# An opening rearranged: three weight tiles in step with the input, products of zeros ahead of it, and the squares of the norm between the splits

## The chip, the core and the metric

The kernel runs on one core of one Trainium2 chip. The metric is the device time of one execution in microseconds (us), taken as the median of several runs. The core has a tensor engine (PE) for matrix products, a vector engine (DVE) and a scalar engine (ACT) for elementwise work, and a sync engine (SP) that here only issues transfers (DMA). Each engine works through its own queue strictly in order and waits at an instruction whose input is not there yet.

## The reference, cut to what matters

A state-space mixer (SSD) and an attention mixer (MLA) stand one after the other over 512 tokens of 1024 channels, each with a norm ahead and a residual sum behind, in 32-bit floats.

```python
def rms_norm(x, w):
    xf = x.astype(jnp.float32)
    return (xf * lax.rsqrt(jnp.mean(xf * xf, axis=-1, keepdims=True) + RMS_EPS)).astype(x.dtype) * w
...
def ssd_mixer(u, in_w, conv_w, conv_b, dt_bias, a_log, d_skip, norm_w, out_w):
    proj = u @ in_w
    z = proj[..., :SSM_D_INNER]
    xbc = proj[..., SSM_D_INNER:SSM_D_INNER + SSM_CONV_DIM]
    dt_raw = proj[..., SSM_D_INNER + SSM_CONV_DIM:]
    xbc = jax.nn.silu(causal_depthwise_conv(xbc, conv_w, conv_b)).astype(jnp.float32)
    ...
    dt = jax.nn.softplus(dt_raw.astype(jnp.float32) + dt_bias.astype(jnp.float32))
    a = dt * (-jnp.exp(a_log.astype(jnp.float32)))
    y = ssd_chunked(xs * dt[..., None], a, b_in, c_out)
    y = y + d_skip.astype(jnp.float32)[:, None] * xs
    y = gated_group_rms_norm(y.reshape(bsz, seq, SSM_D_INNER), z, norm_w, SSM_N_GROUPS)
    return y.astype(u.dtype) @ out_w
...
def reference(x, norm_w, ...):
    h = x
    for i in range(DEPTH):          # layer 0: ssd_mixer, layer 1: mla_mixer
        u = rms_norm(h, norm_w[i])
        ...
        h = h + y.astype(h.dtype)
    return rms_norm(h, final_norm_w)
```

## The kernel before

**Tiling.** Channels lie on the 128 partitions and the 512 tokens along the rows, so the input is eight tiles `x[k]` of 128 x 512. The input projection is cut into tiles of 128 output channels; the weights of one tile are 128 x 1024 (eight blocks k of 128 x 128). Every 32-bit operand is split in two parts, a rounded one (`hi`, a cast on ACT) and the rest (`lo`, a subtraction on DVE), and each product is made of three: hi by hi, hi by lo, lo by hi. One projection tile is therefore 8 x 3 = 24 matrix products of 128 x 512.

**Norm.** The norm's factor is the same for all channels of a token, so group 0's projections, and the first four of group 1, are made from `vh`, `vl`, the parts of x times the norm's weight, and multiplied by the factor `r` afterwards. `sumsq` makes `r`: eight squares on ACT (`sq`), summed on DVE (`sqa`), split (`sqh`, `sql`), summed over the partitions by two products with ones (`pssq`), then logarithm, exponential and three DVE steps (`rstd_of`, tile `rr`).

**Groups.** The state-space mixer has eight groups g. The six projection tiles of a group are called B, C, x0, x1, z0 and z1. `ssm_in` makes them, `ssm_evac` applies `r` and the convolution (three shifted multiply-adds, the "taps"), and class `SSD` makes scores (`cb`, `L`), weighted inputs (`xdt`, `xw`), states (`S`) and outputs (`y`). While the group's state-space work runs, the projections of the next group run on PE: the method `sched` weaves small pieces into the stream of products at places given by a table of numbers, in units of PE work. PE's order is thus the order in which the code is written and woven; the order on ACT, DVE and SP is set by a scheduler from the program and its own estimates.

**Weights.** `prefetch` loads a tile's raw weights (pool `wraw`, two buffers, 512 KB each, by SP), and splits them (`whi`, `wlo`, pools of three) up to two tiles ahead. A load waits until the tile that had its buffer is split; a cast into `whi` waits until PE is done with the tile three before. I count weight tiles from 0 in the order of use: 0 to 5 are group 0's, 6 to 11 are group 1's.

**Step sizes (`ssm_dt`).** Sixteen products with the small matrix `wdt` make the raw step sizes (`aux`); times `r` they are `d0`; four products with the identity turn them ("transposes"); then softplus on DVE; then four products that make cumulative sums, copied by ACT to `acT`, stored to DRAM (`ac_d`) and loaded back spread over partitions (`L<-ac_d`).

**The opening.** SP loads `x[0]`, then the first pieces of weight tiles 0 and 1, `x[1]`, `x[2]`, the second pieces, and so on. ACT and DVE split as pieces land; `gemm2` runs tiles 0 and 1 (B and C) in step with the input: per k six products. Then follows tile 2 (x0): six of its products, the sixteen for the step sizes, the two of `pssq`, its other eighteen, and then the four transposes of `d0`. The `link` call in `sumsq` holds all squares back until the last `vh` is made.

Of the kernel before, what the change touches and what calls it, by code (L numbers as in the profile page):

```python
# [33 lines left out]

# Where work is woven into the stream of matrix products, in units of tensor-engine work done since the
# start of the stream (of its share, for SC, TU and PR).
S0P = (13.82, 14.2, 15.4, 15.6, 17.62)  # group 0's projections: dt projection, norm, softplus, raw tiles, cumulative sums
SU = (0.64, 1.42)  # start and spacing of the normalised input tiles
P0 = (6.0, 6.8, 11.91, 15.25, 17.25, 24.88, 32.86, 35.86)  # group 0: sums, decays, cb, x0, x1, states, y0, y1
P1 = (1.0, 2.4, 3.8, 12.0, 16.5, 21.0)  # later groups: cb, x0, x1, states, y0, y1  # L40
GN = 16.84  # gated norm of the group before
G7 = 33.0  # gated norm of the last group
SF = (0.02, 0.1, 2.1, 3.1)  # scores of head 0
SC = (0.0, 0.16, 0.25, 0.44)  # scores of the next head
TU = (0.02, 0.08, 0.38, 0.55)  # transposes of a head's probabilities
PR = (0.3, 0.48, 0.65, 0.94)  # products of a head's probabilities and values
KO = (3, 4, 5, 8, 10)  # steps of the output projection given to the last heads
MID = 4  # projections of group 1 that still use the input without its norm
NU = 1  # projection after which the second norm is worked out
LA = (3, 1)  # heads of a group whose decay exponents the scalar engine takes: groups 0-1, later ones  # L50
OA = 8  # tiles that the output projection splits ahead
SQ = 2


# [88 lines left out]
class Net:  # L143
# [113 lines left out]
    def split_weight(self, raw, cuts=()):  # L257
# [8 lines left out]
        yield hi, lo  # L266

    def mm(self, n=T):
        return self.ps.tile([P, n], F32, tag="mm", name=self.nm("mm"), bufs=3)
# [16 lines left out]
    def gemm2(self, ps, ws, xh, xl, ks):  # L286
        seqs = [self.passes(w, xh, xl, ks) for w in ws]
        for k in range(ks):
            for p, seq in zip(ps, seqs):
                for i in range(3 * k, 3 * k + 3):  # L290
                    self.nc.tensor.matmul(p, seq[i][0], seq[i][1], start=i == 0, stop=i == 3 * ks - 1)  # L291
            yield 6 * 0.216

# [34 lines left out]
    def sumsq(self, tiles, n, pstag, pool=None, tags=("r0", "rt", "rr"), after=None):  # L328
        nc = self.nc
        acc = None  # L330
        for x in tiles:
            sq = self.nrm.tile([P, T], F32, tag="sq", name=self.nm("sq"), bufs=SQ)
            i = nc.scalar.activation(sq[:], x, AF.Square)
            if after is not None:
                self.link(i, [after])
            if acc is None:
                acc = self.nrm.tile([P, T], F32, tag="sqa", name=self.nm("sqa"))
                nc.vector.tensor_scalar(acc[:], sq[:], self.eps_of(n), None, op0=ALU.add)
            else:
                nc.vector.tensor_tensor(acc[:], acc[:], sq[:], op=ALU.add)  # L340
# [10 lines left out]
    def ssm(self):  # L351
# [9 lines left out]
        self.link(self.head, [ld])  # L361
        self.phase, self.group = "E", [self.head]
        raws = [self.wraw.tile([P, D], F32, tag="raw", name=self.nm("raw")) for _ in range(2)]
        self.wload = 2
        for k in range(KD):
# [3 lines left out]
            if k % 2 == 0:  # L369
                s = slice(k * P, (k + 2) * P)  # L370
                for i, raw in enumerate(raws):
                    nc.sync.dma_start(raw[:, s], t["w"][i, :, s])
        wdt = wk.tile([P, KD, NH], F32, name="wdt", bufs=1)
# [9 lines left out]

        vh, vl = [], []
        ws = [self.split_weight(raw, (256, 512, 768)) for raw in raws]
        for k in range(KD):
            a = self.o16.tile([P, T], F32R, tag="o", name=self.nm("vh"))
            b = self.o16.tile([P, T], F32R, tag="o", name=self.nm("vl"))
            last = nc.scalar.activation(a[:], self.xs[k][:], AF.Copy, scale=nw[:, k:k + 1])
            if k % 2 == 0:  # L390
# [6 lines left out]
        for i, w in enumerate(ws):  # L397
            self.wready[self.wq[i]] = next(w)
        self.wpos = 2
        self.ssd_aux = aux  # L400
        box, self.wait = [], []

        def norm0():
            pss = self.sumsq([x[:] for x in self.xs], D, "aux", after=last)
            box.append(self.rstd_of(pss, D))
# [150 lines left out]
    def ssm_in(self, g, uh, ul, early):  # L556
# [3 lines left out]
        for i, (name, ct) in enumerate((("B", 16 + g), ("C", 24 + g), ("x0", 2 * g), ("x1", 2 * g + 1),  # L560
                                        ("z0", 0), ("z1", 0))):
            pair = (0, 1) if g == 0 and i < 2 else (4, 5) if g == NG - 1 and i >= 4 else None
            w = None if pair and i == pair[1] else self.weight("w", U_IN + 6 * g + i)
            xh, xl, r = early[:3] if i < early[3] else (uh, ul, None)
# [5 lines left out]
            if pair:  # L570
                if i == pair[0]:
                    two = [ps, self.mm()]
                    ws = [w, self.weight("w", U_IN + 6 * g + i + 1)]
                    yield from self.gemm2([p[:] for p in two], ws, xh, xl, KD)
                ps = two[i - pair[0]]
            else:
                yield from self.gemm(ps[:], w, xh, xl, KD)
# [486 lines left out]
```

## Time and profile before

| what | value |
|---|---|
| time of the kernel before, median of 3 runs | 843.92 us (843.35 to 844.57) |
| the profiled execution, first to last instruction (span) | 841.8 us |
| what lies around that span, against the median | 2.1 us |
| PE busy in the span | 825.0 us (98%) |
| DVE busy | 641.1 us (76%) |
| ACT busy | 453.2 us (54%) |
| mean granted clock of PE | 0.997 |

The profile has the span of one execution only; its own time as a whole is not in it, so the median less the span, 2.1 us, is taken for what lies around. Rows of a timeline read: start, duration, engine, line, operation, what is written from what, tile size, count, and in brackets the engine's idle time just before and what ended it. In a row of several, the duration is that of the whole row. Two rows that follow each other on one engine overlap by some tens of nanoseconds, since an instruction's record begins before the one ahead has left the engine; so what one costs in a stream is the distance of two starts and not its own duration.

### The profile page before, as it was taken

What the parts mean: (1) busy time and instruction counts of PE and PEld (TensorE: products, weight loads), DVE (VectorE), ACT (ScalarE), POOL (GpSimd) and SP (SyncE); (2) the same over time, 40 slices, a digit from 0 to 9 for tenths busy, and PEclk for the clock granted to TensorE, in tenths of its full rate; (3) what the DMA queues carried; (4) which work ended last, traced back from release to release, by engine and by line L of the source; (5) the groups of instructions that cost most, each with busy time, mean ns of one, the idle gap of its engine ahead of it and who ended that gap; (6) DMA issues with size and microseconds to landing.
All of it is one profiled execution on the core that took longest, in us unless ns stands there. A gap on an engine that the chain in (4) does not pass through costs nothing.

```text
span 841.8 us, 11569 instructions
## 1 busy us (share of the span) xinstructions
PE 825.0 (98%) x4260; PEld 694.9 (83%) x4260; DVE 641.1 (76%) x1226; ACT 453.2 (54%) x802; POOL 0.2 (0%) x4
## 2 busy tenths in 40 slices
PE   6999999999999999999999999999999999999996
PEld 5887888888888888888888888888888888888885
DVE  6999898888887979877465787776867869675544
ACT  7567755545455647334354564457547557553233
POOL 0000000000000000000000000000000000000000
PEclk9999999999999999999999999999999999999998
DMA  6354533434332424332224332122221224321212
GB/s 225 104 175 152 160 131 113 124 122 127 104 126 101 150 76 125 113 122 82 99 100 152 102 116 75 56 86 66 77 65 54 88 71 162 100 93 59 89 62 100
DMA packets 35112, 90.55 MB, mean 108 GB/s; under 512 B 4784, under 2 KB 6320, under 8 KB 35056
## 3 DMA queue, kind: packets, MB, share of 16 engines
q1 hardware_dynamic: 34336, 88.77, 32.6%
q10 hardware_dynamic: 720, 1.05, 0.3%
q8 instruction: 33, 0.54, 0.3%
q14 instruction: 23, 0.19, 0.1%
HBM read 83.12 MB, written 4.33 MB: 104 GB/s over the span
## 4 chain that ended last, share of the span: by engine, by line
PE 90%; DVE 4%; DMA 3%; ACT 2%; issue 1%; SPq 0%; DVEq 0%; ACTq 0%
PE mm L282 53%; PE ot L934 10%; PE s L786 5%; PE mm L291 4%; PE po L828 4%; PE mm L766 3%; PE pt L810 2%; PE yd L132 2%; PE yo L127 1%; PE aux L105 1%; DMA x<-in_x_dram 1%; PE aux L77 1%; PE aux L89 1%; PE yd L282 1%; PE yo L282 1%
## 5 line engine op out<-in xcount | busy, mean ns | idle before, releaser
L263 ACT CAST whi<-raw 128x1024 fp32r<-128x1024 f32 (+3 forms) x132 | 126.9, 965 | 178.7 <-PE mm L282 141.7
L264 DVE TENSOR_TENSOR wlo<-raw,whi 128x1024 fp32r<-128x1024 f32 (+3 forms) x132 | 146.8, 1115 | 52.0 <-ACT whi L263 51.8
L282 PE MATMUL mm<-ah,whi 128*128 128x512 f32 x384 | 153.8, 400 | 0.0
L282 PE MATMUL mm<-ah,wlo 128*128 128x512 f32 x384 | 150.1, 391 | 0.4 <-DVE wlo L264 0.4
L282 PE MATMUL mm<-al,whi 128*128 128x512 f32 x384 | 149.7, 390 | 0.0
L282 PE MATMUL mm<-vh,whi 128*128 128x512 f32 x224 | 89.6, 400 | 1.6 <-ACT whi L263 1.6
L282 PE MATMUL mm<-vh,wlo 128*128 128x512 f32 x224 | 87.8, 392 | 0.7 <-DVE wlo L264 0.7
L282 PE MATMUL mm<-vl,whi 128*128 128x512 f32 x224 | 87.5, 390 | 0.0
L282 PEld LDWEIGHTS mm<-ah,wlo 128*128 128x128 f32 x384 | 72.1, 188 | 16.1 <-DVE wlo L264 0.8
L282 PEld LDWEIGHTS mm<-ah,whi 128*128 128x128 f32 x384 | 72.2, 188 | 15.2 <-issue 1.0
L282 PEld LDWEIGHTS mm<-al,whi 128*128 128x128 f32 x384 | 72.2, 188 | 14.4 <-DVE al L303 0.3
L934 PE MATMUL ot<-whi,ah 128*128 128x512 f32 (+1 forms) x136 | 52.3, 384 | 0.0
L934 PE MATMUL ot<-whi,al 128*128 128x512 f32 (+1 forms) x136 | 51.4, 378 | 0.0
L934 PE MATMUL ot<-wlo,ah 128*128 128x512 f32 (+1 forms) x136 | 51.4, 378 | 0.0
L282 PEld LDWEIGHTS mm<-vh,wlo 128*128 128x128 f32 x224 | 42.0, 188 | 10.8 <-DVE wlo L264 1.5
L282 PEld LDWEIGHTS mm<-vh,whi 128*128 128x128 f32 x224 | 42.1, 188 | 10.0 <-ACT whi L263 1.8
L214 ACT ACTIVATE p<-p,st 128x128 f32<-128x128 f32 (+1 forms) x64 | 36.1, 564 | 25.0 <-DVE st L798 24.8
L282 PEld LDWEIGHTS mm<-vl,whi 128*128 128x128 f32 x224 | 42.2, 188 | 7.2
L814 ACT CAST ph<-pt 128x512 fp32r<-128x512 f32 (+1 forms) x64 | 26.4, 421 | 33.5 <-PE pt L810 33.1
L282 PE MATMUL mm<-ch,whi 128*128 128x512 f32 x104 | 42.6, 409 | 0.0
L282 PE MATMUL mm<-ch,wlo 128*128 128x512 f32 x104 | 40.8, 393 | 0.0
L282 PE MATMUL mm<-cl,whi 128*128 128x512 f32 x104 | 40.7, 392 | 0.0
(231 smaller groups left out, 1649.0 us busy)
## 6 DMA issues: line engine op xcount, KB each, us to landing
raw<-in_w_dram SPq DMA_DIRECT2D x100, 512.0 KB, 3.2
L<-ac_d SPq DMA_DIRECT2D x32, 256.0 KB, 4.1
E<-ea_d SPq DMA_DIRECT2D x32, 128.0 KB, 3.2
raw<-in_ua_dram SPq DMA_DIRECT2D x8, 512.0 KB, 3.3
raw<-in_ub_dram SPq DMA_DIRECT2D x8, 320.0 KB, 2.9
x<-in_x_dram SPq DMA_DIRECT2D x8, 256.0 KB, 4.5
res<-in_x_dram SPq DMA_DIRECT2D x8, 256.0 KB, 3.1
hd<-ht SPq DMA_DIRECT2D x8, 256.0 KB, 2.4
```

The costliest lines, as they stand in the source:

```text
L132: nc.tensor.matmul(yd[64 * h:64 * h + 64, s], self.xdt[j][:, c, h, :], self.L[2 * j + h][:, s], start=True, stop=True)
L214: i = self.nc.scalar.activation(out, in_, func, **k)
L263: nc.scalar.copy(hi[:, a:b], raw[:, a:b])
L264: nc.vector.tensor_tensor(lo[:, a:b], raw[:, a:b], hi[:, a:b].bitcast(F32), op=ALU.subtract)
L282: self.nc.tensor.matmul(ps, a, b, start=i == 0, stop=i == len(seq) - 1)
L291: self.nc.tensor.matmul(p, seq[i][0], seq[i][1], start=i == 0, stop=i == 3 * ks - 1)
L766: nc.tensor.matmul(ps[:, c2 * 256:(c2 + 1) * 256], a, b, start=i == 0, stop=i == 5)
L786: nc.tensor.matmul(ps[:, :n], x[:, s], y[:, :n], start=k == 0, stop=k == 4)
L810: nc.tensor.transpose(pt[:, (b - kb) * P:(b - kb + 1) * P], probs[h][b][:, kb * P:(kb + 1) * P], self.ident)
L814: nc.scalar.copy(ph[:, :n], pt[:, :n])
L828: nc.tensor.matmul(po[:, kb * P:], x, y, start=kb == 0 and k == 0, stop=kb == NCH - 1 and k == 2)
L934: nc.tensor.matmul(ps[:, a:b], x, y, start=start and i == 0, stop=stop and i == 5)
```

## The change

Four things change, all in the opening; the tables that weave the work, S0P among them, stay.

- A tile `idle` of 128 x 128 zeros is written by DVE at the start, and PE multiplies it by itself seven times into a buffer that nobody reads, ahead of everything else.
- Weight tile 2 joins tiles 0 and 1: four more loads of 128 KB stand among the first on SP (its raw data lies in tiles of the pool `act` that are free then), four more narrow splits on ACT and DVE, and `gemm2` now runs three tiles in step, nine products for each k. The wide load and split of tile 2 go.
- The squares of the norm are each linked to the `vh` three later instead of the last one, so they can stand among the splits.
- The cost that `gemm2` reports for a step is now by the number of tiles. The pieces of table S0P fall due where that sum passes them.

```diff
+WARM = 7
...
+    def split_first(self, raw):
+        nc = self.nc
+        hi = self.whi.tile([P, D], F32R, tag="hi", name=self.nm("whi"))
+        lo = self.wlo.tile([P, D], F32R, tag="lo", name=self.nm("wlo"))
+        for k, part in enumerate(raw):
+            s = slice(2 * k * P, 2 * (k + 1) * P)
+            nc.scalar.copy(hi[:, s], part)
+            nc.vector.tensor_tensor(lo[:, s], part, hi[:, s].bitcast(F32), op=ALU.subtract)
+            yield
+        yield hi, lo
...
-            yield 6 * 0.216
+            yield 3 * len(ws) * 0.216
...
-        for x in tiles:
+        for k, x in enumerate(tiles):
...
-                self.link(i, [after])
+                self.link(i, [after[k]])
...
+        idle = wk.tile([P, P], F32, name="idle", bufs=1)
+        nc.vector.memset(idle[:], 0.0)
+        pw = aux()
+        for _ in range(WARM):
+            nc.tensor.matmul(pw[:, :P], idle[:], idle[:], start=True, stop=True)
         raws = [self.wraw.tile([P, D], F32, tag="raw", name=self.nm("raw")) for _ in range(2)]
-        self.wload = 2
+        raws = [[raw[:, 2 * k * P:2 * (k + 1) * P] for k in range(KD // 2)] for raw in raws]
+        third = [self.act.tile([P, T], F32, tag=g, name=self.nm("raw")) for g in ("ah", "al")]
+        raws.append([third[k // 2][:, (k % 2) * 2 * P:(k % 2 + 1) * 2 * P] for k in range(KD // 2)])
+        self.wload = 3
...
-                    nc.sync.dma_start(raw[:, s], t["w"][i, :, s])
+                    nc.sync.dma_start(raw[k // 2], t["w"][i, :, s])
...
-            pss = self.sumsq([x[:] for x in self.xs], D, "aux", after=last)
+            pss = self.sumsq([x[:] for x in self.xs], D, "aux", after=[marks[min(k + 3, KD - 1)] for k in range(KD)])
...
-            pair = (0, 1) if g == 0 and i < 2 else (4, 5) if g == NG - 1 and i >= 4 else None
-            w = None if pair and i == pair[1] else self.weight("w", U_IN + 6 * g + i)
+            pair = (0, 1, 2) if g == 0 and i < 3 else (4, 5) if g == NG - 1 and i >= 4 else None
+            w = None if pair and i != pair[0] else self.weight("w", U_IN + 6 * g + i)
...
-                    two = [ps, self.mm()]
-                    ws = [w, self.weight("w", U_IN + 6 * g + i + 1)]
+                    two = [ps] + [self.mm() for _ in pair[1:]]
+                    ws = [w] + [self.weight("w", U_IN + 6 * g + k) for k in pair[1:]]
```

How the rows move is shown at three places. Line numbers are those of each kernel's own file, so they differ by 12 to 20 between the two; a word in brackets names the engines or transfers whose signals a row waits for. First PE, at the end of the opening: `pssq` is the sum of squares over partitions, `d` is `d0`, `mm_246` is tile 2 (x0), `yd` tile 3 (x1). Before:

```order
L347 MATMUL pssq_306<-sqh_302,onesr 128x512 [waits Activation_49]
L348 MATMUL pssq_306<-sql_303,onesr 128x512 [waits DVE_49]
L282 MATMUL mm_246<-vh_146,whi_188 128x512
...
L282 MATMUL mm_246<-vh_178,wlo_189 128x512
L495 MATMUL aux_358<-ident,d_323 128x128 [waits DMAHW2_49,DVE_49]
L495 MATMUL aux_358<-ident,d_323 128x128 x3
L282 MATMUL yd_400<-vh_130,whi_242 128x512
```

and now:

```order
L507 MATMUL aux_296<-vl_205,w_291 128x512
L359 MATMUL pssq_344<-sqh_340,onesr 128x512 [waits Activation_49]
L360 MATMUL pssq_344<-sql_341,onesr 128x512 [waits DVE_49]
L515 MATMUL aux_371<-ident,d_355 128x128 [waits DMAHW6_49,DVE_49,PE_49]
L515 MATMUL aux_371<-ident,d_355 128x128 x3
L294 MATMUL yd_420<-vh_146,whi_215 128x512
```

The eighteen products of tile 2 that stood between `pssq` and the transposes of `d0` now stand ahead of both; nothing stands between any more. (The number of rows and their order behind the transposes are the same in both, down to the second group's products.)

Second ACT, at the logarithm that begins `r` (`r<-pssq`). Before, one wide cast (tile 4) stood between `sqh` and it; now two do, those of tiles 4 and 5 (`whi_416`, `whi_454`), the second of which waits for its own load:

```order
L264 CAST whi_215<-raw_211 128x1024 [waits DMAHW2_49,PE_49]
L356 CAST sqh_340<-sqa_315 128x512 [waits DVE_49]
L264 CAST whi_416<-raw_213 128x1024 [waits DMAHW3_49,PE_49]
L264 CAST whi_454<-raw_414 128x1024 [waits DMAHW4_49,PE_49]
L215 ACTIVATE r_56_347<-pssq_344 128x512 [waits PE_49]
```

Third DVE, at the split of tile 10 (z0 of group 1): `L` and `cb` are the scores of group 0, `x` and `xdt` the taps and weighted inputs. Before:

```order
L626 TENSOR_SCALAR L_638<-L_638,ac 128x128 [waits DMAHW0_49,DVE_49]
L626 TENSOR_SCALAR L_638<-L_638,ac 128x128 x3
L79 TENSOR_TENSOR cb_713<-aux_708,con 128x512 [waits PE_49]
L264 TENSOR_TENSOR wlo_749<-raw_677,whi_748 128x1024 [waits DMAHW7_49,Activation_49]
L81 TENSOR_TENSOR L_617<-L_617,cb_713 128x512 [waits DVE_49,Activation_49]
L81 TENSOR_TENSOR L_624<-L_624,cb_713 128x512 [waits Activation_49]
```

and now:

```order
L82 TENSOR_TENSOR L_658<-L_658,cb_733 128x512
L622 SCALAR_TENSOR_TENSOR x_134_751<-raw_752,cols,x_134_751 128x511 [waits Activation_49]
L93 TENSOR_TENSOR xdt_763<-aux_758,dt 128x512 [waits PE_49]
L622 SCALAR_TENSOR_TENSOR x_134_751<-raw_752,cols,x_134_751 128x510 [waits DVE_49]
L95 TENSOR_TENSOR xw_665<-xdt_763,dec 128x3x128 [waits DVE_49]
L622 SCALAR_TENSOR_TENSOR x_134_751<-raw_752,cols,x_134_751 128x509 [waits DVE_49]
L265 TENSOR_TENSOR wlo_769<-raw_697,whi_768 128x1024 [waits DMAHW3_49]
```

The `lo` part of tile 10 has moved back past the four `L` products, the three taps of x0, one `xdt` and one `xw`. PE's products of that tile stand where they stood, and the third of them reads `wlo`.

More of the change, by code (lines that the diff above doesn't have):

```diff
@@ L382, in ssm @@
         nc.vector.tensor_copy(self.onesr[:], self.ones)
-        vh, vl = [], []
-        ws = [self.split_weight(raw, (256, 512, 768)) for raw in raws]
+        vh, vl, marks = [], [], []
+        ws = [self.split_first(raw) for raw in raws]
         for k in range(KD):
@@ L388, in ssm @@
             b = self.o16.tile([P, T], F32R, tag="o", name=self.nm("vl"))
-            last = nc.scalar.activation(a[:], self.xs[k][:], AF.Copy, scale=nw[:, k:k + 1])
+            marks.append(nc.scalar.activation(a[:], self.xs[k][:], AF.Copy, scale=nw[:, k:k + 1]))
             if k % 2 == 0:
@@ L398, in ssm @@
             self.wready[self.wq[i]] = next(w)
-        self.wpos = 2
+        self.wpos = 3
         self.ssd_aux = aux
```

## The prediction

> **What bounds the kernel now.** First the page's first part and the list of what PE waited for in the first 110 us:
>
> ```profile
> span 841.8 us, 11569 instructions
> PE 825.0 (98%) x4260; PEld 694.9 (83%) x4260; DVE 641.1 (76%) x1226; ACT 453.2 (54%) x802; POOL 0.2 (0%) x4
> ...
> PE mm L291 <- ACT whi L263: 4.8, 1, 4.8
> ...
> PE yo L127 <- DVE E L135: 0.2, 1, 0.2
> PE aux L495 <- DVE d L491: 0.2, 1, 0.2
> ```
>
> PE bounds the whole; a change in the opening counts by what it does to PE's idle time there and as far as its wake reaches. Then the timeline of PE in the opening, and the chain that ended last, from `pssq` on:
>
> ```profile
> 4.78 0.80 PE L291 MATMUL mm<-vh,whi 128*128 128x512 f32 x1 [4.78 <-ACT whi L263]
> 7.15 0.63 PE L291 MATMUL mm<-vh,wlo 128*128 128x512 f32 x1
> 7.58 0.59 PE L291 MATMUL mm<-vh,whi 128*128 128x512 f32 x1
> 8.00 0.40 PE L291 MATMUL mm<-vl,whi 128*128 128x512 f32 x1
> 8.24 0.40 PE L291 MATMUL mm<-vh,wlo 128*128 128x512 f32 x1
> 18.92 0.50 PE L282 MATMUL mm<-vh,whi 128*128 128x512 f32 x1 [1.41 <-ACT whi L263]
> 20.18 0.50 PE L282 MATMUL mm<-vh,wlo 128*128 128x512 f32 x1 [0.53 <-DVE wlo L264]
> ...
> 25.25 0.24 PE pssq L348
> 25.52 0.61 ACT r L214
> ...
> 28.99 0.70 DVE d L491
> ...
> 29.73 0.66 PE aux L495 x4
> 30.39 5.46 PE yd L282 x24
> ```
>
> Products start 0.43 us apart until 8.00 and 0.23 after it: PE begins at half speed. It loses 1.94 us at tile 2's wide split (1.41 and 0.53). From `pssq` to the end of `d0` it takes 29.69 - 25.52 = 4.17 us, in which PE works on the eighteen products of tile 2 and idles 0.16. A product in the stream costs 5.46 / 24 = 0.2275.
>
> Behind that, DVE sets the pace, as its rows show:
>
> ```profile
> 29.60 1.87 DVE L598 TENSOR_TENSOR raw<-mm,rr 128x512 f32<-128x512 f32 x3
> 31.39 0.74 DVE L602 SCALAR_TENSOR_TENSOR B<-raw,cols,B 128x511 f32<-128x511 f32 x1
> 32.05 0.74 DVE L602 SCALAR_TENSOR_TENSOR C<-raw,cols,C 128x511 f32<-128x511 f32 x1
> 37.74 1.21 DVE L264 TENSOR_TENSOR wlo<-raw,whi 128x1024 fp32r<-128x1024 f32 x1
> 38.87 0.21 DVE L510 TENSOR_SCALAR dy<-de 128x128 f32<-128x128 f32 x1
> 62.89 0.74 DVE L417 SCALAR_TENSOR_TENSOR u<-x,cols,rr 128x512 f32<-128x512 f32 x1
> 65.64 0.88 DVE L626 TENSOR_SCALAR L<-L,ac 128x128 f32<-128x128 f32 x4 [2.01 <-DMA L<-ac_d]
> 67.04 1.21 DVE L264 TENSOR_TENSOR wlo<-raw,whi 128x1024 fp32r<-128x1024 f32 x1
> ```
>
> It works without a pause of note from 29.60 to 63.63, waits 2.01 for `L`, and goes on; the 67.04 row is tile 10. PE meets that queue here:
>
> ```profile
> 72.88 0.39 PE L282 MATMUL mm<-ah,wlo 128*128 128x512 f32 x1
> 79.21 1.56 PE L105 MATMUL aux<-xw,BT 128*128 128x256 f32 x6 [1.19 <-DVE xw L94]
> 81.61 0.50 PE L282 MATMUL mm<-ah,wlo 128*128 128x512 f32 x1 [0.37 <-DVE wlo L264]
> ```
>
> 72.88 is the product that reads tile 10's `lo`: made by 68.2, it is early by 4.7 us. Behind 100 us PE waits for almost nothing.
>
> **The change, part by part.** *The opening.* The first input and weight piece are ahead of all else as before, so real work still starts at 4.78. The zeros are seven products of 128 columns in full 32-bit floats, of which four (eight records, since each runs in two) are this row:
>
> ```profile
> 53.37 1.05 PE L531 MATMUL aux<-con,a 128*128 128x128 f32 x8
> ```
>
> So they take 1.8 us, or 3.7 at half speed, and PE's 4.8 us of waiting at the start covers them, as DVE's idleness there covers the writing of the tile: they cost nothing, and if they lift the clock the 0.43 spacing goes. To the end of `pssq` PE now has 72 + 16 + 2 = 90 products, 90 x 0.2275 = 20.5, so 25.3 if nothing is late. Late is the second input tile, by one piece of 128 KB, which takes 0.4 us at the rate of these slices:
>
> ```profile
> 6.00:7.00 1.00, 1.00 (x4) 0.81 (x3) 0.14 (x1) 0.90 (x2) 0.00 (x0) 1.00 1.04 351
> ```
>
> and then its `vh` and `vl` (0.7 each): nine fast products of k = 0 are done before that, which I put at 0.9 us of waiting. From then on a pair of k brings 0.92 MB, 2.6 us at that rate, for 18 products of 4.1 us: PE is ahead no more. `pssq` ends at 26.2 (25.3 without the wait; if the zeros don't help, 3.2 us at half speed cost 1.5, of which 0.9 hides in the wait: 26.8). Squares and sums end near 21.3 and don't hold it.
>
> *The chain to d0.* The 1.94 of tile 2 is gone, but the eighteen products that covered the 4.17 are ahead of `pssq` now, so all of it is bare. And the logarithm stands on ACT behind tile 5's cast, whose load waits until tile 3 is split, which waits until PE is done with tile 0:
>
> ```profile
> 19.30 1.03 ACT L263 CAST whi<-raw 128x1024 fp32r<-128x1024 f32 x1
> 20.24 1.15 ACT L333 ACTIVATE sq<-x 128x512 f32<-128x512 f32 x2
> ...
> raw<-in_w_dram SPq DMA_DIRECT2D x100, 512.0 KB, 3.2
> raw<-in_w_dram SPq DMA_DIRECT2D x5, 512.0 KB, 4.0
> ```
>
> PE leaves tile 0 after 66 products: 4.78 + 0.9 + 66 x 0.2275 = 20.7; cast 0.95 (20.24 - 19.30), split 1.13 (38.87 - 37.74): 22.8; load 3.2 to 4.0, I take 3.6, the middle of the two rows: 26.4; cast: 27.4. So the logarithm starts at 27.4 and not at 26.2, and `d0` ends at 27.4 + 4.17 = 31.6 against 29.69: **1.9 us later** (without the gate 30.4). PE stands still for 5.4 us.
>
> *The queue of DVE to tile 10.* From the end of `d0` PE needs 72.88 - 29.69 = 43.2 us to the product that reads tile 10's `lo`, and the order of PE's rows there is unchanged. DVE has to do, up to and with that split: 29 scalar-tensor-tensor operations of some 512 columns (taps and `u`) at 32.05 - 31.39 = 0.66, 19.1; 5 wide splits at 1.13, 5.7; 23 tensor-tensor operations at 0.61 (1.87 for three overlapped ones), 14.0; the softplus chain and other small ones, 6.0; the `L` row 0.8; one `xw` 0.5. Sum 46.1. The same prices give 33.8 for the work from 29.60 to the end of the row at 62.89, measured 33.95. Add 0.9 of waits for ACT, which before were filled with the taps of x0 and two splits: 47.0. Then `L`:
>
> ```profile
> 54.62 0.58 ACT L535 COPY acT<-aux 128x512 f32<-128x512 f32 x1
> 55.23 3.88 DMA ac_d<-acT
> 56.32 0.68 DVE L598 TENSOR_TENSOR raw<-mm,rr 128x512 f32<-128x512 f32 x1
> ```
>
> `acT` began 24.9 after `d0`; now it stands on ACT behind B's cast, which waits for that `raw` row, at 25 in the new queue, so 25.8; and the store stands behind one more 512 KB load (up to 1.5 us). `L` came 35.95 after `d0`; I take 36.8 to 38.3, against DVE's arrival at 36.2: 0.6 to 2.1 of waiting, 1.2 taken. Tile 10's `lo` is ready 47.0 + 1.2 = 48.2 after `d0`, PE needs it after 43.2: **a new wait of 5.0 us** (0.4 of it already at the cumulative sums, for `acT`). It ends at 31.6 + 48.2 = 79.8, against 72.88: PE is 6.9 late.
>
> *What that wait absorbs.* The waits at `xw` (1.19), tile 11's split (0.37) and `yo` (0.18) vanish, since DVE is through with them when PE arrives: -1.7. One split (tile 14) now stands ahead of the first `y` and can hold the second `yd` for 0 to 0.6: +0.3. PE's later work is unchanged.
>
> Sum: 6.9 - 1.7 + 0.3 = **+5.5 us**: a span of 847.3, and with the 2.1 around it (843.92 less 841.8) **849.4**. Lower bounds (no waiting in the opening, no gate, `L` and ACT in time, 0.5 off the queue): `d0` at 29.5, 45.6 behind it, 75.1, so 2.2 - 1.7 = +0.5. Upper: `d0` 32.5, queue 49.1, +0.6, one cold clock: +9.1.
>
> **The rivals.** *The clock falls in the gaps.* At the end of the program the clock halves after the last product:
>
> ```profile
> 833.67 0.28 PE L934 MATMUL ot<-wlo,ah 128*128 128x256 f32 x1
> 836.00:837.00 1.00, 0.00 (x0) 0.00 (x0) 0.77 (x3) 0.67 (x2) 0.00 (x0) 1.00 0.07 29
> 837.00:838.00 1.00, 0.00 (x0) 0.00 (x0) 0.00 (x0) 0.17 (x1) 0.00 (x0) 0.72 1.02 375
> ```
>
> 0.72 is a fall at 837.44, 3.5 us after the last product's end. The gaps of 5.4 and about 5 are longer. A cold start costs 3.2 us at 0.43, 1.5 us; behind the first gap it only shortens the second wait, behind the second it adds: 850.9. [...] From the rows alone: one gap of that length stands in the trace, at the end, and there the clock fell; but only a fall behind the second gap costs, and its 4.6 at the split itself is not much over 3.5. I give this 0.23.
>
> *A lighter queue.* No gate on the logarithm (a load that lands in 3.2 behind an early tile 3) and `L` in time: `d0` 30.4, 47.0, so 77.4 and +3.1: 847.0. For it: idle DMA at 22 us; against: tile 5's cast is ahead in the order whatever the load does. 0.17.
>
> *Faster.* DVE reaches tile 10's split within 43 us of `d0`, so that PE never waits there. Then only the start counts: +0.7 (no gate) - 1.7 = -1.0: 842.9. It decides if the 47.0 is 4 too many, which the 0.15 error of the check speaks against; for it, DVE has nothing else to do while `d0` is late. 0.05.
>
> *The zeros don't lift the clock.* `pssq` and what hangs on it 0.6 later: 850.0. 0.06.
>
> **How the numbers follow.** Likeliest 849.4, chance 0.49; its own range 847.6 to 851.2. A measurement here tells 0.2%, 1.7 us, from no change. Slower by more: 0.49 + 0.23 + 0.17 + 0.06 less 0.03 for their lower ends, 0.92; within: 0.04; faster 0.04. The range for eight in ten reaches from the lighter queue with some of its bounds to the cold clock: 845.5 to 852.5.
>
> **What would show it.** In the profile after: products 0.23 apart from 4.8 on; no wait at a wide split near 19; a wait of some 5 us at the transposes of `d0` (released by DVE `d`), the logarithm behind ACT's cast and not `pssq`; a wait of 4 to 5 us near 75, released by DVE `wlo`; none at `xw`. It is wrong if the transposes run before 30.4, if DVE's split of tile 10 ends less than 44 us after `d0`, or if PE's rows turn out to be woven otherwise.

## The result, and the profile after

The changed kernel takes 852.18 us (median of 4 runs, 851.36 to 853.46) against 844.25 (843.35 to 845.19) of the kernel before on the same chip: a ratio of 1.0096, 95% interval 1.0083 to 1.0109, that is 7.9 us slower. The prediction was 849.4, in a range from 845.5 to 852.5. The profiled execution took 852.48 us, its span is 850.7 against 841.8.

The page of the kernel after begins:

```profile
span 850.7 us, 11606 instructions
PE 832.4 (98%) x4274; PEld 702.0 (83%) x4274; DVE 642.5 (76%) x1230; ACT 454.0 (53%) x805; POOL 0.2 (0%) x4
```

PE is busy for 7.4 us more than before: 3.4 of them are the zeros, in time in which PE waited before, and the rest is PE at half clock (granted clock 0.50 from 30.87 to 37.69 and from 82.07 to 85.48, and products 0.43 us apart for longer at the start), since no other product was added. What PE waited for up to 110 us, after (line and operation, releaser, us in total, times, longest):

```profile
PE aux L515 <- issue: 5.1, 1, 5.1
PE mm L294 <- DVE wlo L265: 3.5, 1, 3.5
...
PE yd L133 <- DVE y L138: 0.5, 1, 0.5
```

The two waits that the prediction named are there, at the transposes of `d0` (5.1; "issue" means that the profile shows no releaser, but the wait ends 0.1 us behind `d0`, and in e3 it is put down to DVE `d`) and at tile 10's `lo` (3.5). The waits at tile 2's split, at `xw`, at tile 11 and at `yo` are gone. The timeline of PE, after:

```profile
1.05 3.36 PE L379 MATMUL aux<-idle 128*128 128x128 f32 x14 [1.05 <-DVE eps L334]
4.90 0.80 PE L303 MATMUL mm<-vh,whi 128*128 128x512 f32 x1 [0.50 <-ACT whi L275]
...
9.82 0.63 PE L303 MATMUL mm<-vh,wlo 128*128 128x512 f32 x1
10.25 0.48 PE L303 MATMUL mm<-vh,whi 128*128 128x512 f32 x1
10.57 0.39 PE L303 MATMUL mm<-vl,whi 128*128 128x512 f32 x1
...
27.82 0.40 PE L360 MATMUL pssq<-sql,onesr 128*128 128x512 f32 x1
33.36 1.08 PE L515 MATMUL aux<-ident,d 128*128 128x128 f32 x4 [5.14 <-issue]
...
78.29 0.39 PE L294 MATMUL mm<-al,whi 128*128 128x512 f32 x1
82.15 0.79 PE L294 MATMUL mm<-ah,wlo 128*128 128x512 f32 x1 [3.47 <-DVE wlo L265]
82.74 0.63 PE L294 MATMUL mm<-ah,whi 128*128 128x512 f32 x1
83.17 0.63 PE L294 MATMUL mm<-al,whi 128*128 128x512 f32 x1
...
88.82 1.46 PE L106 MATMUL aux<-xw,BT 128*128 128x256 f32 x6
```

Products of the opening stay 0.43 apart until 10.25 and not until 8.00 as before, in spite of the zeros, and they are 0.43 apart once more behind the second wait. The timeline of ACT, after:

```profile
28.16 1.04 ACT L264 CAST whi<-raw 128x1024 fp32r<-128x1024 f32 x1 [3.07 <-DMA raw<-in_w_dram]
29.11 0.59 ACT L215 ACTIVATE r<-pssq 128x512 f32<-128x512 f32 x1
```

and of DVE, after:

```profile
32.57 0.69 DVE L511 TENSOR_TENSOR d<-aux,rr 128x512 f32<-128x512 f32 x1
...
71.57 0.88 DVE L646 TENSOR_SCALAR L<-L,ac 128x128 f32<-128x128 f32 x4 [1.03 <-DMA L<-ac_d]
...
73.62 0.68 DVE L618 TENSOR_TENSOR raw<-mm,rr 128x512 f32<-128x512 f32 x1
...
80.88 1.22 DVE L265 TENSOR_TENSOR wlo<-raw,whi 128x1024 fp32r<-128x1024 f32 x1
```

The logarithm stands behind tile 5's cast, and `d0` ends at 33.3. From 73.62 to 80.88 DVE does 7.3 us of work that the kernel before did behind that split; tile 10's `lo` is ready at 82.1, 48.8 after `d0` (38.6 before: 68.25 less 29.68).

All of it adds up at one instruction, the product that reads `xw` (L106; L105 before). From its start to the end of the span it is 762.6 us before and 761.9 after. It starts at 88.82 in place of 79.21, +9.61: the transposes are 3.63 later (33.36, 29.73); from them to tile 10 PE needs 45.32 in place of 43.15 with its clock at 0.50 from 30.87 to 37.69, +2.17; the wait is 3.47; from there to L106 it needs 6.67 in place of 5.14, at 0.50 from 82.07 to 85.48, +1.53; and the wait of 1.19 at `xw` is gone.

### The profile page after: what moved, and what is told of

Its sections match the earlier page's. It is cut to its first block, busy times and chain, and to the rows that moved or that the text cites. A ratio compares the mean times of both kernels' runs of the same rounds, so it can differ in the third digit from the quotient of the medians.

```text
span 850.7 us, 11606 instructions
## 1 busy us (share of the span) xinstructions
PE 832.4 (98%) x4274; PEld 702.0 (83%) x4274; DVE 642.5 (76%) x1230; ACT 454.0 (53%) x805; POOL 0.2 (0%) x4
## 4 chain that ended last, share of the span: by engine, by line
PE 89%; DVE 5%; DMA 2%; ACT 2%; issue 1%; SPq 0%; ACTq 0%; DVEq 0%
PE mm L294 51%; PE ot L954 10%; PE mm L303 6%; PE s L806 5%; PE po L848 3%; PE mm L786 2%; PE pt L830 2%; PE yd L133 2%; PE aux L106 1%; PE yo L128 1%; DVE wlo L265 1%; PE yd L294 1%; PE aux L78 1%; PE aux L90 1%; DVE x L622 1%
## 5 line engine op out<-in xcount | busy, mean ns | idle before, releaser
L264 ACT CAST whi<-raw 128x1024 fp32r<-128x1024 f32 (+2 forms) x123 | 123.0, 1001 | 188.7 <-PE mm L294 141.8
L265 DVE TENSOR_TENSOR wlo<-raw,whi 128x1024 fp32r<-128x1024 f32 (+2 forms) x123 | 142.6, 1161 | 60.2 <-ACT whi L264 60.0
L294 PE MATMUL mm<-vh,whi 128*128 128x512 f32 x216 | 86.3, 399 | 0.0
L294 PE MATMUL mm<-vh,wlo 128*128 128x512 f32 x216 | 84.6, 392 | 0.1
L294 PE MATMUL mm<-vl,whi 128*128 128x512 f32 x216 | 84.4, 391 | 0.0
```

The lines of the kernel that those rows point to most:

```text
L264: nc.scalar.copy(hi[:, a:b], raw[:, a:b])
L265: nc.vector.tensor_tensor(lo[:, a:b], raw[:, a:b], hi[:, a:b].bitcast(F32), op=ALU.subtract)
L294: self.nc.tensor.matmul(ps, a, b, start=i == 0, stop=i == len(seq) - 1)
```

## The experiments

Each was run beside the kernel before. From its own trace come the end of `d0`, the place of tile 10's split on DVE (counted in instructions from `d0`), the end of that split, the wait of PE for it, and the start of L106 (the line's number shifts by a few between kernels). Times are medians.

| kernel | time, us | ratio (95%) | `d0` | place | split ends | wait | L106 |
|---|---|---|---|---|---|---|---|
| before (first 3 runs; 843.8 to 844.3 beside the others) | 843.92 | | 29.7 | 65 | 68.3 | 0 | 79.2 |
| after | 852.18 | 1.0096 (1.0083–1.0109) | 33.3 | 81 | 82.1 | 3.5 | 88.8 |
| after, again (e10) | 852.19 | 1.0100 (1.0086–1.0113) | 32.5 | 81 | 82.0 | 4.5 | 89.8 |
| split early (e1) | 847.44 | 1.0037 (1.0025–1.0049) | 31.9 | 68 | 74.3 | 0 | 84.0 |
| cover (e2) | 846.32 | 1.0026 (1.0017–1.0035) | 32.1 | 63 | 69.0 | 0 | 81.4 |
| no zeros (e3) | 853.80 | 1.0125 (1.0109–1.0141) | 33.7 | 81 | 83.2 | 3.8 | 90.0 |
| two tiles (e4) | 844.87 | 1.0010 (1.0002–1.0019) | 31.9 | 65 | 69.8 | 0 | 80.8 |
| logarithm first (e5) | 852.72 | 1.0105 (1.0092–1.0118) | 31.6 | 81 | 80.9 | 4.1 | 88.9 |
| e5, split behind `d0` (e11) | 844.99 | 1.0015 (1.0006–1.0024) | 31.0 | 60 | 67.0 | 0 | 81.0 |
| two tiles, dt first (e6) | 841.82 | 0.9975 (0.9965–0.9984) | 29.2 | 65 | 66.9 | 0 | 77.8 |
| e6, split behind `d0` (e9) | 850.53 | 1.0083 (1.0070–1.0097) | 28.1 | 83 | 79.2 | 3.2 | 87.0 |
| e9, split asked early (e12) | 843.36 | 0.9995 (0.9987–1.0004) | 27.9 | 66 | 66.8 | 0 | 78.4 |
| zeros only (e7) | 842.75 | 0.9992 (0.9983–1.0000) | 29.4 | 65 | 66.4 | 0 | 77.6 |
| squares only (e8) | 845.21 | 1.0019 (1.0010–1.0027) | 30.4 | 65 | 69.2 | 0 | 80.1 |

In every trace L106 to the end of the span is 761.1 to 763.3 us, so to within some 2 us what an experiment does to the time is what it does to that start. "The planner" in the expectations is the scheduler that sets the order on ACT, DVE and SP.

### Tile 10's split in its old place (e1_early_split)

```diff
                 at = P0[2:]
+                pieces.append((11.0, lambda: self.prefetch(11)))
```

> The changed kernel, with one piece added that asks for tile 10's split while the products of tile 8 run, so that in VectorE's order the split comes 13 rows earlier (it leaves the four products of L with cb, C's and x0's taps and two splits of the normalised input behind it). Nothing else moves on TensorE. My theory (the order of VectorE's queue behind d0 sets a second wait, and the clock falls in it): some 7 us less stand ahead of the split, so that it ends near 75 in place of 82.1; TensorE is there at 78.7 and does not wait; the 3.5 us wait and the cold products behind it (1.8) go; the waits at xw return with about 0.5. Time 846.5 to 848. Rival (VectorE as a whole is behind by that much, whatever its order): the wait only moves to the products that read xw, S or y, and the time stays at 851 to 853. Rival (the loss is the 5.1 us at the transposes and nothing else): 852, with TensorE's second wait gone but the same amount lost elsewhere.

847.44, as the first theory had it. What PE waited for, e1:

```profile
PE aux L516 <- issue: 5.2, 1, 5.2
...
PE aux L106 <- DVE xw L95: 0.2, 1, 0.2
```

and the split on DVE, e1:

```profile
73.08 1.22 DVE L265 TENSOR_TENSOR wlo<-raw,whi 128x1024 fp32r<-128x1024 f32 x1
```

The first gap is as long as ever; the second is gone, and 4.7 us with it. PE's order is that of after, and near the split little else moved: its cast on ACT and a few neighbours. So this run is the cleanest measure of what the split's place costs. Some 3 us are left against the kernel before, with the late `d0` and the bare gap, which this run keeps. The rival that VectorE's lateness only moves elsewhere falls for most of it: small waits come back at `cb` (0.8), `S` (0.5) and `xw` (0.2).

### Work between pssq and the transposes (e2_cover)

```diff
-S0P = (13.82, 14.2, 15.4, 15.6, 17.62)
+S0P = (13.82, 14.2, 15.4, 15.6, 24.0)
```

> The changed kernel with the last number of S0P at 24.0 in place of 17.62: the transposes of d0 are put behind all 24 products of tile 3 (yd) in place of ahead of them, so that these products stand between pssq and the transposes, as tile 2's do in the kernel before. The planner then also puts tile 10's split 22 rows earlier in VectorE's order. My theory: d0 still ends near 33.3; TensorE works from 28.2 to 33.7 and its 5.1 us wait goes, with the half clock behind it; it comes to tile 10 near 72.5 to 74, and the split is ready near 72 to 73, so that the second wait is below 1 us; time 843.5 to 846. Rival (VectorE's work behind d0 sets the end whatever TensorE does ahead of it): the second wait grows by the 5 us that the first loses, and the time stays at 851 to 853. Rival (the first gap costs its 5.1 us and the second wait stays): 846.5 to 848 with a wait of 3 us or more at tile 10.

846.32, a little over the expected range. What PE waited for, e2:

```profile
PE aux L551 <- DVE a L545: 3.7, 1, 3.7
...
PE aux L106 <- DVE xw L95: 0.7, 1, 0.7
```

The 5.1 at the transposes is gone, but 3.7 comes back at the cumulative sums: with the transposes asked for later the scheduler puts softplus behind the taps of x0 and x1. L106 starts 7.4 earlier than after, and tile 10's split, 18 instructions nearer to `d0`, is part of it; so this run changes two things at once.

### Without the zeros (e3_no_zeros)

```diff
-WARM = 7
+WARM = 0
```

> The changed kernel without the seven products of zeros (the tile is still written); TensorE has nothing to do until the first input. My theory after the traces (the zeros lift no clock; the clock rises at the end of the first of its windows that real products fill): same time as with them, 851 to 853, products 0.43 us apart for 3 to 7 us from 4.8 on. Rival (the zeros fill part of a window and bring the rise forward by one window of 3.4 us on average in some runs): 1 to 1.5 us slower, 853 to 854. Rival (the zeros are in the way): faster.

853.80, the number of the first rival: some 2 us between the two ratios (1.0125 and 1.0096, whose intervals just touch). PE, e3:

```profile
7.54 0.63 PE L303 MATMUL mm<-vh,whi 128*128 128x512 f32 x1
7.96 0.50 PE L303 MATMUL mm<-vl,whi 128*128 128x512 f32 x1
...
26.70 0.40 PE L360 MATMUL pssq<-sql,onesr 128*128 128x512 f32 x1
```

and ACT, e3:

```profile
22.36 0.62 ACT L356 CAST sqh<-sqa 128x512 fp32r<-128x512 f32 x1 [1.37 <-DVE sqa L352]
22.89 2.00 ACT L264 CAST whi<-raw 128x1024 fp32r<-128x1024 f32 x2
28.56 1.04 ACT L264 CAST whi<-raw 128x1024 fp32r<-128x1024 f32 x1 [3.67 <-DMA raw<-in_w_dram]
```

But this trace does not show that the zeros are the reason. The clock rose at 8.2, behind a window from 4.76 that was 3.42 us busy, and 2.2 us earlier than in after, and `pssq` ended at 27.1, 1.1 earlier; `d0` came 0.4 later all the same. Without the zeros the scheduler put tile 3's cast behind `sqh` (22.89 is the casts of tiles 3 and 4), so tile 5's load came no earlier with the products, and the logarithm stood 2.4 us behind `pssq` in place of 0.9 (at 29.51: ACT, idle from 24.89, first took the cast ahead of it in its queue, at 28.56). The run changes two things, and what the zeros bring in the changed kernel stays open.

### Two tiles in step (e4_two_tiles)

```diff
-            pair = (0, 1, 2) if g == 0 and i < 3 else ...
+            pair = (0, 1) if g == 0 and i < 2 else ...
-        third = ...
-        raws.append(...)
-        self.wload = 3
+        self.wload = 2
-        self.wpos = 3
+        self.wpos = 2
```

> The changed kernel with two tiles in step in place of three: tile 2 is loaded whole and computed behind the pair as in the kernel before, its last 18 products behind pssq; the zeros, the squares among the splits and the loads in pieces stay. My theory (the third tile in step takes the cover from the chain to d0, and through VectorE's order makes the second wait; zeros and squares cost nothing): 843 to 845.5, no wait of over 1 us at the transposes. Rival (the squares among the splits or the zeros delay the opening): 846 or more, with d0 later than 31. Rival (the squares early are a gain by themselves): below 843.

844.87: taking back the third tile takes back 7 of the 8 us. On DVE tile 10's split has its old place, and L106 starts at 80.8. PE at tile 2's split, e4:

```profile
20.23 0.79 PE L294 MATMUL mm<-vh,whi 128*128 128x512 f32 x1 [2.24 <-ACT whi L264]
```

The clock fell in this wait of 2.24 us, and the granted clock was 0.50 from 20.06 to 23.47, which no theory had.

### The parts alone on the kernel before (e7_zeros_only, e8_squares_only)

```diff
+        idle = wk.tile([P, P], F32, name="idle", bufs=1)
+        nc.vector.memset(idle[:], 0.0)
+        pw = aux()
+        for _ in range(7):
+            nc.tensor.matmul(pw[:, :P], idle[:], idle[:], start=True, stop=True)
```

> The kernel before with the seven products of zeros added and nothing else. My theory (zeros count as work for the clock: it rises at the end of the first of its 3.41 us windows that is filled to more than some 80%, which is between 4 and 7 us with them and near 8 without, except where the window's edge falls badly): products 0.23 us apart from 4 to 7 us on; the wait for tile 2's split grows by part of what is won, since it is set by loads and ScalarE; time 843 to 844.3, that is 0 to 1 us faster. Rival (zeros do nothing for the clock): the same time, products 0.43 us apart until 8. Rival (the longer wait at tile 2 then lets the clock fall): up to 1.5 us slower.

842.75: zeros bring some 0.7 us by the ratio, anything from nothing to 1.4 by its interval. The clock rises at 5.2, and the wait for tile 2's split is 1.26 + 0.53. The 80% was an estimate: in the traces the clock did not rise behind windows 2.51 and 2.91 us busy of 3.41 (after; 74% and 85%) and rose behind one of 2.92 (e2).

```diff
-                self.link(i, [after])
+                self.link(i, [after[k]])
```

with the marks of the change as `after`.

> The kernel before with the squares of the norm tied to the input three tiles on, as in the change, in place of all behind the last one; nothing else. My theory (the squares are not what pssq waits for, in either kernel; earlier they only share ScalarE and VectorE with the splits): 843.5 to 845, pssq within 0.6 us of 25.25. Rival (the squares hold up pssq, so that it comes earlier now): d0 1 us or more earlier, 842 to 843. Rival (they delay the splits that the pair waits for): pssq a microsecond or more later, 845 to 846.

845.21, 1.6 us slower by the ratio (0.8 to 2.3), so the second rival was the better one: ACT begins tile 2's cast at 18.52 in place of 17.84, with two more squares ahead of it, and `d0` ends 0.7 later. PE, e8, where a wait of 1.41 stood before:

```profile
19.60 0.50 PE L282 MATMUL mm<-vh,whi 128*128 128x512 f32 x1 [1.77 <-ACT whi L263]
```

### The logarithm ahead of tile 5's cast (e5_log_first, e11_log_first_split_behind)

```diff
+            if self.wpos == 5:
+                self.link(c, [self.last])      # c: the cast; last: the exponential of r
```

> The changed kernel with one order forced on ScalarE: tile 5's cast stands behind the two steps of the norm (logarithm, exponential) in place of ahead of them, so that the logarithm waits for pssq alone. My theory (the cast gates the logarithm by about 0.9 us, and VectorE's queue, which starts with d0, carries every delay of d0 to tile 10): d0 ends 3.6 to 4.2 us after the end of pssq in place of about 5.1, the wait at the transposes falls from 5.1 to about 4.2, and the time by 0.9: 850.5 to 852 beside some 852.5 of the changed kernel. Rival (the queue behind d0 is held by ScalarE or by L, so that d0 earlier by 0.9 brings nothing): no change, the wait at tile 10 unchanged at its clock time.

852.72, no gain. DVE, e5:

```profile
28.44 0.69 DVE L328 TENSOR_TENSOR rt<-rt,r 128x512 f32<-128x512 f32 x1
29.05 1.22 DVE L267 TENSOR_TENSOR wlo<-raw,whi 128x1024 fp32r<-128x1024 f32 x1
30.19 0.68 DVE L329 SCALAR_TENSOR_TENSOR rr<-rt,r 128x512 f32<-128x512 f32 x1
```

The logarithm started 0.03 behind `pssq`, but the same tile's split on DVE now stood between two steps of the norm and took 1.1 us back. So that split was sent behind `d0` too:

```diff
+            if self.wpos == 5:
+                self.link(v, [self.d0])        # v: the subtraction; d0: the product that makes d0
```

> The changed kernel with two orders forced: on ScalarE tile 5's cast behind the logarithm and the exponential, as in the experiment with the logarithm first, and on VectorE tile 5's split behind d0 in place of between the norm's second and third step, where it stood in that experiment (29.05, 1.2 us). My theory (that split took back what the logarithm had won): d0 ends 4.1 to 4.3 us after the end of pssq in place of 5.1 to 5.2, the wait at the transposes is 4.2, and the time is 0.8 to 1.2 below that of the changed kernel, near 851.3. Rival (the queue behind d0 is held by ScalarE or by L, not by d0): d0 earlier, the wait at tile 10 longer by as much, no gain.

844.99, where I had expected 851.3. `d0` ended 4.2 us behind `pssq`, as expected, 0.6 earlier than in e5. What my expectation left out is the order further down: the scheduler had put tile 10's split 21 instructions nearer to `d0`, ahead of the four products of `L` with `cb`. What PE waited for, e11:

```profile
PE aux L519 <- issue: 4.3, 1, 4.3
```

and the split on DVE, e11:

```profile
65.77 1.22 DVE L267 TENSOR_TENSOR wlo<-raw,whi 128x1024 fp32r<-128x1024 f32 x1
```

A kernel with three tiles in step, zeros, squares and a gap of 4.3 us is 1.2 us slower than the kernel before, once that split stands ahead of the `L` products again. Of the 7.7 us between e5 and e11, 0.6 is `d0`, 4.1 the wait at the split, and some 3 the half clock behind it (0.50 from 80.08 to 86.90 in e5). Many other rows of DVE and ACT differ between the two, so this pair alone does not single the split out; e1 does that.

### The dt projection behind the pair (e6_two_dt_first, e9_dt_first_split_behind, e12_split_asked_early)

Two tiles as in e4, and:

```diff
-S0P = (13.82, 14.2, 15.4, 15.6, 17.62)
+S0P = (10.3, 14.2, 15.4, 15.6, 17.62)
```

> Two tiles in step as in the experiment with two tiles, with the first number of S0P at 10.3 in place of 13.82: the sixteen products of the dt projection run right behind the pair, and tile 2 behind them, so that its split has 3.6 us more, and six of its products stand ahead of pssq and eighteen behind. My theory (what counts in the opening is when d0 ends and that TensorE has work until then; everything up to the states hangs 49 us of VectorE's work behind d0): the 2.2 us wait for tile 2's split and the half clock behind it go, pssq comes at 23.5 to 25 and d0 ends at 27.7 to 29.2 against 29.69 before and 31.8 with two tiles; time 841.5 to 843.5, faster than both kernels. Rival (the squares or the dt weights are not ready earlier, so that pssq stays near 27): 844 to 845, with a wait of about 2 us at the dt projection or at pssq.

841.82, 0.25% faster than the kernel before (0.16 to 0.35%) and 1.2% faster than the change: the fastest version here. The sixteen products of the dt projection fill the time in which tile 2 is split, and the logarithm starts at 23.99 in place of 25.52. The timeline of PE, e6:

```profile
29.26 0.63 PE L513 MATMUL aux<-ident,d 128*128 128x128 f32 x4 [1.21 <-issue]
...
77.83 1.56 PE L106 MATMUL aux<-xw,BT 128*128 128x256 f32 x6 [0.27 <-DVE xw L95]
```

and of DVE, e6:

```profile
26.62 1.22 DVE L265 TENSOR_TENSOR wlo<-raw,whi 128x1024 fp32r<-128x1024 f32 x1
27.75 0.68 DVE L327 SCALAR_TENSOR_TENSOR rr<-rt,r 128x512 f32<-128x512 f32 x1
```

Here too a split stands between two steps of the norm. Sending it behind `d0` (the link of e11, for tile 4) was to bring that microsecond:

> The kernel with two tiles in step and the dt projection right behind them, with one order forced on VectorE: the split of tile 4, which ran between the second and the third step of the norm there (26.62, 1.2 us), stands behind d0. My theory (all up to the states hangs on the end of d0; a split between the norm's steps delays it by its own 1.14 us): d0 ends near 27.9 in place of 29.1, the 1.2 us wait at the transposes goes, and the time falls by 0.7 to 1.2: 840.5 to 841.5 beside 841.8. Rival (the split is then late for tile 4's products, or the load of the next tile is): a wait of about 1 us at tile 4, no gain. Rival (TensorE's rate is the bound now): no gain, no wait.

850.53, 8.7 us slower than e6 though `d0` ends 1.1 earlier. What PE waited for, e9:

```profile
PE mm L296 <- DVE wlo L265: 3.2, 1, 3.2
PE yo L296 <- DVE wlo L265: 2.7, 1, 2.7
```

From the link the scheduler made another order: tile 4's split 15 instructions behind `d0`, and tile 10's 83, behind `L` and the taps, just as in the change. This is the counterpart of e11: the two-tile opening with no gap at the transposes (0.2) has the second wait all the same. With tile 4's split asked for right behind `d0`,

```diff
+ [(15.45, lambda: self.prefetch(5))]
```

> The kernel of the experiment before (two tiles in step, the dt projection behind them, tile 4's split behind d0), with tile 4's split asked for by a piece of its own at 15.45, right behind the step that makes d0, so that it takes the first place behind d0 on VectorE. The planner then also puts tile 10's split back ahead of the four products of L with cb, at row 96 of VectorE in place of behind them. My theory (the 8 us are the place of tile 10's split in VectorE's order, in the changed kernel as in that experiment): the waits of 2.7 at tile 4 and 3.2 at tile 10 and the half clock behind both go, d0 still ends near 28.1, and the time is 840.5 to 842, at or just below the 841.8 that the two tiles with the dt projection first took. Rival (d0 ahead of its old place is what disturbs the queue, or the load of tile 10 is late): a wait of 3 us or more at tile 10 and 848 to 851 again.

843.36: both waits go and 7.2 us come back, but `d0` 1.2 earlier than in e6 brings nothing. What PE waited for, e12:

```profile
PE aux L106 <- DVE xw L95: 2.0, 1, 2.0
```

`xw` is ready at 78.4, in e6 at 77.8: DVE had another order again. And behind the wait of 2.05 the granted clock was 0.50 from 78.59 to 82.00.

### The changed kernel once more (e10_after_again)

> The changed kernel itself, once more, for a second trace. My theory (the edges of the clock's 3.41 us windows fall anywhere; in the first trace a window with the idle 0.5 us between zeros and work and thin first products was 2.91 us busy, by the trace's own busy time, and the clock rose only at 10.4, while in five other kernels with zeros it rose between 4.0 and 6.5): the clock rises between 4 and 7 with a chance of some three in four, d0 then ends at 31.7 to 32.2 in place of 33.3, the wait at tile 10 is 3.3 to 4.3, and the span is 849 to 850; otherwise again near 10, with d0 at 33 and a span near 850.7. Rival (zeros in this kernel do not count): the rise at 7.5 to 10.5 again and d0 at 33. Median of the times 851.5 to 853 either way.

852.19 against 852.18. The clock rose at 9.1: not between 4 and 7 as I gave the better chance, and `d0` ended at 32.5. PE's busy time between the edges at which the clock changed tells more. All changes of the clock that a trace records lie whole multiples of 3.413 us apart (in after at 10.39, 30.87, 37.69, 82.07 and 85.48; from the first to the fourth 71.68 us, 21 x 3.413), and cut at such edges a trace gives windows of 3.41 us. Columns: window, its length, PE busy and instructions, further engines, then the granted clock (1.00 stands also where nothing is recorded yet), the DMA share and GB/s. After:

```profile
0.15:3.56 3.41, 2.51 (x12) 2.52 (x12) 0.19 (x4) 1.28 (x1) 0.20 (x4) 1.00 0.39 130
3.56:6.97 3.41, 2.91 (x9) 2.18 (x9) 1.81 (x4) 2.03 (x5) 0.00 (x0) 1.00 0.88 265
...
27.45:30.87 3.42, 0.77 (x4) 0.28 (x2) 1.64 (x2) 2.17 (x3) 0.00 (x0) 1.00 0.53 158
```

After again (e10):

```profile
2.24:5.66 3.42, 2.97 (x13) 2.44 (x11) 1.09 (x2) 1.46 (x4) 0.00 (x0) 1.00 0.79 236
...
26.14:29.55 3.41, 1.42 (x7) 0.82 (x5) 1.05 (x1) 2.10 (x3) 0.00 (x0) 1.00 0.64 217
...
80.75:84.16 3.41, 2.09 (x5) 1.70 (x6) 3.41 (x6) 1.44 (x2) 0.00 (x0) 0.50 0.32 92
```

Behind the windows of 2.91 and 2.97 us in which zeros end and work begins the clock did not rise; in e7 the same window has 2.97, and behind it the clock rose:

```profile
1.82:5.24 3.42, 2.97 (x14) 2.57 (x12) 0.70 (x2) 1.64 (x3) 0.00 (x0) 1.00 0.89 198
```

Of the eleven profiled executions with zeros the clock rose at 4.0 to 6.9 in eight and at 9.1 to 10.4 in three (after, e9, e10); without zeros (before, e3, e8) at 8.0 to 8.7. In e2 it rose behind a window that holds zeros alone, before any other product ran:

```profile
0.54:3.96 3.42, 2.92 (x13) 2.92 (x14) 0.19 (x4) 1.56 (x2) 0.00 (x0) 1.00 0.52 161
```

So zeros alone were enough in e2. In these eleven, whether they helped went with where an edge fell; in three the clock rose no earlier than without them.

## Why the prediction was right, and where its sizes were off

The measured 852.2 lies 0.3 under the top of the range: the two waits came where they were predicted and one of the rivals came with them, while the forecast itself was 2.8 too low.

*The opening: mis-sized.* The prediction had `pssq` end at 26.2, or at 26.8 "if the zeros don't help". It ended at 28.2 in the profiled execution and at 27.6 in e10, and at 26.4 to 26.9 in e1, e2, e5 and e11, where the clock rose by 6.5. PE was the only limit (no wait from 4.90 on); the price of zeros that don't help was taken as 3.2 us at half speed, from the kernel before, and was 5.5 and 4.2. The sign that the prediction gave, products 0.23 apart from 4.8 on, was not there.

*The chain to `d0`: right.* The logarithm began 0.9 behind `pssq`, released by tile 5's cast, and from there to the end of `d0` it was 4.15 us (predicted 4.17). `d0` at 33.3 is 1.7 later than the predicted 31.6 (and later than the 32.5 of the upper bound), all of it the opening: PE left tile 0, which starts the chain to tile 5's load, at 22.6 and not at 20.7. In e1, with a clock that rose in time, it was 31.9. That the gate is worth 0.9 by itself e11 shows (4.2 from `pssq` to `d0`), e5 that lifting it on one engine is not enough.

*The queue of DVE: right.* 48.8 us from `d0` to tile 10's `lo` against 48.2, of which 1.03 waiting for `L` against 1.2. That last term is close by some luck: DVE was there 37.3 after `d0` and not 36.2, and `L` came at 38.3, the late end of what was given. PE came 2.2 later than its 43.2, so the wait was 3.5 and not 5.0; the half clock behind the first gap shortened it, as the prediction said it would. What the prediction took as given, the new place of the split, is the largest part of the loss: 4.7 of 7.9 us by e1. Where the split stood 60 to 68 instructions behind `d0`, in eight variants and the kernel before, there was no wait at it; in the five with 81 to 83 it was 3.2 to 4.5. e1 and e11 take it away with three tiles in step, e9 makes it without. The prediction priced the rows one by one and did not say that the 10.2 us by which the queue grew are the scheduler's order and not work that the change adds: seventeen instructions that stood behind the split now stand ahead of it (7.3 us of them from 73.62 on), and tile 5's split, 1.1 us, went ahead of `d0`.

*What is absorbed: right.* The waits at `xw`, tile 11 and `yo` are gone, the one at the second `yd` is 0.5 (0.3 predicted).

*The rival of the clock: it happened.* Its 850.9 is nearer than the forecast; the upper end of the range had one such fall in it. It was given 0.23 on the ground that the second gap is hardly longer than the 3.5 us after which the clock fell at the program's end. The clock fell behind the second gap in all five traces that have that wait. One such fall cost 1.5 us in the trace of after, as priced, and 2.55 in e10, where the clock did not rise behind a second window, 2.09 us busy. A fall did not need those 3.5 us: in e4 it came in a wait of 2.24 us, in e12 behind one of 2.05. By the windows of 3.41 us, the clock fell behind some with up to 1.45 us of work in them (e9; 1.42 in e10, 1.34 in e4, 1.36 in e12).

*Lighter queue, faster, zeros alone.* The lighter queue asked for no gate and `L` in time; `L` was late by 1.03 and the gate was there. Faster needed a split within 43 us of `d0`; e1 comes to 42.4, but by another order. The rival that the zeros don't lift the clock (0.06, 850.0) was true of the profiled execution, with a larger price than given.

In sum the forecast of +5.5 holds 1.9 + 5.0 - 1.7 + 0.3; measured in the same terms, on the span of 850.7, it is 3.6 (`d0`) + 3.5 (wait) + 2.2 and 1.5 (half clock) - 1.7 - 0.2 (the rest behind L106) = 8.9. Of the 3.4 us that it missed, 1.7 are the opening, 0.6 the queue, 1.5 the clock, and some 0.5 less came behind.

## What to carry to other kernels

A step moved ahead of its old place frees what it covered: look for what stands bare now, and then for which engine's queue begins with the late result. Where a scheduler sets the order, compare the whole order of the engine that paces the stage, not the edited lines: here a split that slid 16 places back cost 4.7 us in the run that moves little else (e1), and a link or a piece set elsewhere slid it forth and back (e5 and e11, e9 and e12), each time with 7 to 8 us. A gain that a forced order should bring is only real if the order elsewhere stays, and `prefetch` asked for at a place of its own was the way to hold it.

## What the runs showed of the hardware

Within a trace the granted clock changed only at edges whole multiples of 3.413 us apart (in the kernel before at 7.99 and 837.43, 243 times 3.413), which stood at another place in each execution (the first change at 7.99 there, at 10.39 in after, at 9.07 in e10). By PE's busy time in the records (whose ends are modelled), up to 92 us: it fell fifteen times in the fourteen traces, behind windows of 1.45 us (e9) and less, and not behind 1.69 (e11, the row below), 1.85 (e3) or 2.05 (e8); from half speed it did not rise behind 2.51 us or less, rose behind 3.04 and more, and did either between 2.91 and 2.97. The window of e11 that the clock outlasted, and the one behind it that it did not:

```profile
25.14:28.55 3.41, 1.69 (x8) 1.05 (x6) 0.48 (x2) 1.65 (x3) 0.00 (x0) 1.00 0.72 267
28.55:31.96 3.41, 0.83 (x6) 0.82 (x7) 3.31 (x6) 0.81 (x2) 0.00 (x0) 1.00 0.01 2
```

and the fullest one behind which it fell, in e9:

```profile
74.64:78.05 3.41, 1.45 (x7) 0.86 (x5) 3.41 (x7) 2.58 (x4) 0.00 (x0) 1.00 0.00 0
```

So e12's wait of 2.05 us, all of it in one window (75.18 to 78.59, 1.36 us busy), was enough, and 1.41 + 0.53 us split over two, as in the kernel before (2.68 and 2.21 us busy), cost no clock. Where exactly the limits lie, and whether products with zeros count less than others, these traces leave open.
